# Planning a plain product's weight chunks one product earlier, and loading a 512 KB gain row later, in a two-layer encoder

## The chip, the cores and the metric

The kernel runs on one core of one Trainium2 chip. The metric is the device time of one execution in microseconds. Times of a profile are counted from the start of its span. Engine names are those of the profile: PE (TensorE), DVE (VectorE), ACT (ScalarE), POOL (GpSimd), SP (SyncE, which here only issues loads and stores).

## What is computed

A pre-norm encoder of two layers on 512 tokens of width 1024: in layer 0 two attentions side by side, in layer 1 a neighbourhood attention, and after each a squared-ReLU MLP with a hidden width of 4096. A final RMS norm with a gain row follows. The change touches the MLPs and the final norm:

```python
def sq_relu_mlp(h, w_up, w_down):
    u = jax.nn.relu(h @ w_up)
    return (u * u) @ w_down
...
        h = h + sq_relu_mlp(rmsnorm(h, norm_ffn[layer]), ffn_w_up[layer], ffn_w_down[layer])
    return rmsnorm(h, final_norm)
```

## The kernel before

All matrices are float32. Each operand x is split into a high part (a rounded copy, made by ACT) and a low part (x minus the high part, made by DVE), and a product is three matmuls: high x high, high x low, low x high. A weight chunk arrives from memory in a `raw` tile; its halves are `whi` and `wlo`. The pools have four `raw`, three `whi` and four `wlo` buffers.

**Chunks.** `plan` appends a chunk to a list, and `weights(i)` makes what chunk i needs: it issues the loads of all planned chunks up to i + 5 and makes the halves of all planned chunks up to i + 2. It can only look ahead in what is planned. There are three kinds. `chunk` makes `whi` on ACT (L234) and `wlo` on DVE (L224). `summed_chunk` writes minus the rounded weights to `wlo` on ACT (L261), adds the weights to that by an accumulating load from memory on POOL's queue (L263), and makes `whi` on ACT (L266). `seven_chunk` is for the products below: POOL, for some chunks DVE, forms sums of 128-column blocks (L363 to L365), ACT makes `whi` (L369), DVE makes `wlo` (L370).

**Seven-block products** (`Seven`). A 2 x 2 block product is made of seven block products instead of eight; `run` goes over pairs of row blocks, with 21 matmuls of 256 columns (L457 to L459) for each, and then combines the banks on ACT and DVE (L465 to L469).

**The MLP** (`mlp`). The up projection fills `U`, split activations, and `R`, raw ones; it ends with several seven-block products in `stage`. After each, `finish` squares the result on ACT (L1392, L1393). The down projection has a first part, then `product8`: a plain product over the eight tiles of `U` with the matching weight rows, eight 128-column tiles for each chunk, 24 matmuls of 512 columns (L613 to L615). Its first two chunks are of kind `chunk`, the other six `summed_chunk`. While it runs, `convert` splits the raw activations for the seven-block products that come next, four of seven chunks each (the variable m), in which each result is added to the residual `hT` on DVE (L1592).

In layer 1 there is a last product, `down`, over the remaining four tiles (`last_mlp`), in two halves of 512 output columns with two chunks each. It works with tokens on the partitions and ends in the final norm: `weigh` (L1936) multiplies by the gain row `G`, of which every partition holds a copy: one load of 512 KB (L2065).

**Order.** A program is written engine by engine as a scheduler of the tile library puts the instructions, not strictly as the code is written. Each engine works its own list in order. All raw loads and the gain row are on SP's list, where a load that waits for a buffer holds those behind it. Big tiles come from a list of 32 slots: a slot that is freed goes to its end, and one that is taken comes from its front.

Of the kernel before, what the change touches and what calls it, by code (L numbers as in the profile page):

```python
# [8 lines left out]
F32 = mybir.dt.float32  # L9
# [8 lines left out]
D = 1024  # L18
P = 128
# [16 lines left out]
def encoder_kernel(ctx: ExitStack, tc: tile.TileContext, ins, out, dbg=None):  # L36
    nc = tc.nc
    PE, ACT, DVE, POOL, SP = nc.tensor, nc.scalar, nc.vector, nc.gpsimd, nc.sync
# [50 lines left out]
    def ob():  # L89
        return bank("o", 1)  # L90
# [178 lines left out]
    def rows(w, k0, nk):  # L269
        return w[k0 * P : (k0 + nk) * P, :].rearrange("(k p) n -> p k n", p=P)  # L270
# [6 lines left out]
    def plan(*spec, make=None):  # L277
        asked.append((make or chunk, spec))
        return len(asked) - 1
# [247 lines left out]

        return run()

    def product8(w, first, U, evac, eng=None):  # L530


        nk = len(U)
        ids = [plan([(0, D, rows(w, k, 1))], 1, D, None, eng, make=chunk if n < 2 else summed_chunk)
               for n, k in enumerate(first)]

        def run():
            banks = group(4) + group(4)

            def one(k, j):  # L540

                wh, wl = (z[:, 0, P * j : P * j + P] for z in weights(ids[k], AHEAD - (k == 1 or k == nk - 1 and j < 7)))
                x = U[k].pair()
                mm3(banks[j], wh, wl, x[:, 0, :], x[:, 1, :], k == 0, k == nk - 1)


            for js in (range(4), range(4, 8)):
                for k in (0, 1):
                    for j in js:
                        one(k, j)  # L550
                        yield MM3
            U[0].free()
            U[1].free()
            for k in range(2, nk - 2):
                for j in range(8):
                    one(k, j)
                    yield MM3
                U[k].free()
            for j in range(8):
                for k in (nk - 2, nk - 1):  # L560
                    one(k, j)
                    yield MM3

                if j < 5:
                    evac(j, banks[j])
            for j in range(5, 8):
                tc.keep_in_program_order(evac(j, banks[j]))
            U[nk - 2].free()
            U[nk - 1].free()

        return run()
# [775 lines left out]
    SIZES = (6, 8, 16, 2), (6, 8, 14, 4)  # L1347

    def first_product(l):

        w = ins["ffn_w_up"][l]
# [6 lines left out]
        U, R = [], []  # L1358
# [89 lines left out]
        def ahead():  # L1448
            state["ids"] = x7.plan(w, P * state["c"])

        def stage(n, raw=0, more=0):


            at = [], []
            if not state["plain"]:
                plain()
                at[0].extend(range(0, n, 2))
            nu, nr = (n - len(U)) // 2, raw // 2
            state["n"], state["halves"] = n, raw

            kinds = [1, 0] * nu if nr else [0] * nu
            kinds += [1] * (nr + nu - len(kinds)) + [1] * (more // 2)
            for i, kind in enumerate(kinds):
                ids = state["ids"]
                if i < nu + nr:
                    at[kind].append(state["c"])
                state["c"] += 2
                if i < len(kinds) - 1:
                    ahead()
                for u, _ in enumerate(x7.run(ids, (pair_evac, raw_evac)[kind])):  # L1470
                    if u in (14, 21, 24):
                        next(state["late"], None)
            if state["c"] == 32:
                x7.free()
            got = U[:n], R[: raw // 2], R[raw // 2 :], at, state["late"]
            U.clear()
            R.clear()
            return got
# [41 lines left out]
    def mlp(l, last=None, then=lambda: None):  # L1520
# [4 lines left out]
        stage, ahead, later = first_product(l)  # L1525
# [31 lines left out]
                later(c, i)  # L1557
        for s_ in U:
            s_.free()
        U, R, V, (at_u, at_r), late = stage(*SIZES[l][1:])  # L1560
        first = [k + z for k in at_u for z in range(2)]
        gen = product8(w, first, U, ev)
        u7 = Seven(2 * len(R))
        ids = [u7.plan(w, 256 * m, at_r) for m in range(4)]
        k0 = 32 - 2 * len(V)
# [360 lines left out]
    def last_mlp():  # L1926
# [85 lines left out]
        def down(k0, nk, c, up, tail):  # L2012
# [4 lines left out]
            def run():  # L2017
                banks = group(4)
                if c:
                    banks.append(ob())  # L2020

                def use(k, j, o=0, n=S):
                    wh, wl = (x[:, k % 2, o : o + n] for x in weights(ids[k // 2]))
# [26 lines left out]
        def last(k0, R):  # L2050
            up = []
            runs.extend(down(k0, 2 * len(R), c, up, 2 + 2 * c) for c in range(2))

            def beside(m, i):
                if m == 0 and i % 8 == 4 and R:
                    w_ = R.pop(0)
                    for z in range(2):
                        V.append(Slot())
                        up.append(V[-1].pair())
                        split(w_.t[:, S * z : S * z + S], up[-1])  # L2060
                    w_.free()
                if m == 2 and i == 0:
                    H.extend([Halves(spare_p, F32), Halves(spare_p, F32), Halves(spare_b, F32), Slot(F32)])
                    G.append(Slot(F32))
                    SP.dma_start(G[0].t, ins["final_norm"].unsqueeze(0).to_broadcast([P, D]))  # L2065

            return beside

# [59 lines left out]
```

## Time and profile before

| | us |
|---|---|
| median of 3 runs | 1141.09 |
| lowest, highest | 1140.44, 1141.96 |
| the profiled execution, its own time | 1140.78 |
| its span, first to last instruction | 1139.0 |
| mean granted clock of TensorE | 0.998 |

Rows of a timeline give start, duration, engine, line, operation and tile; in brackets stands how long the engine idled before, and what ended it. PE's rows overlap, since matmuls are pipelined: the distance from start to start is the pace. In a view of waits a row is who waited for whom, us in total, how often, and the longest. In a view of DMAs a row gives the transfers of one kind, their number, KB each and the median us from issue to landing.

### The profile page before, as it was taken

The numbers are of one execution on the slowest core, as the hardware profiler recorded it, in microseconds if no ns is written. First come the engines' busy times: TensorE is split into PE (matmuls) and PEld (weight loads), VectorE is DVE, ScalarE is ACT, GpSimd is POOL, SyncE is SP. The second block draws the span as 40 slices with busy tenths as digits, with TensorE's granted clock in tenths as the row PEclk, the third lists the DMA queues.
The fourth block names the chain that finished last, engine by engine and source line by source line (L and its number), as shares of the span: only waits on it lengthen the run. The fifth ranks groups of instructions, "written<-read, shape, count | busy, mean of one in ns | idle before, by whom it ended". The sixth has DMA issues, their size and how long they took to land.

```text
span 1139.0 us, 20506 instructions
## 1 busy us (share of the span) xinstructions
PE 1124.2 (99%) x7348; PEld 1009.6 (89%) x7348; DVE 904.1 (79%) x1570; ACT 668.3 (59%) x1133; POOL 601.3 (53%) x722
## 2 busy tenths in 40 slices
PE   9999999999999999999999999999999999999997
PEld 7787888888899999899998998988889999989996
DVE  6887997988968787969775666667997788697884
ACT  6677785765347668534464555555552666773334
POOL 4366432226688993378532232221388889535740
PEclk9999999999999999999999999999999999999999
DMA  8322441222533235933585574433344233372332
GB/s 240 98 77 77 117 120 62 65 66 74 169 101 100 86 103 134 277 103 103 160 172 157 149 178 130 119 110 121 102 157 130 76 93 94 80 190 74 113 129 74
DMA packets 118325, 136.06 MB, mean 119 GB/s; under 512 B 9923, under 2 KB 99952, under 8 KB 118224
## 3 DMA queue, kind: packets, MB, share of 16 engines
q1 hardware_dynamic: 110736, 119.83, 34.8%
q0 software_dynamic: 7312, 14.83, 6.8%
q8 instruction: 58, 0.95, 0.4%
q14 instruction: 43, 0.35, 0.1%
q10 hardware_dynamic: 176, 0.10, 0.0%
HBM read 112.70 MB, written 6.29 MB: 104 GB/s over the span
## 4 chain that ended last, share of the span: by engine, by line
PE 82%; DVE 7%; issue 6%; DMA 2%; ACT 2%; POOL 1%; SPq 0%; DVEq 0%; POOLq 0%; ACTq 0%
PE mm L613 9%; PE mm L614 8%; PE mm L615 8%; PE mm L459 3%; PE s L1138 3%; PE mm L457 3%; PE mm L458 3%; PE o L1126 3%; PE t L457 2%; PE t L459 2%; PE t L458 2%; PE t L1113 2%; PE s L615 2%; PE s L613 2%; PE s L614 2%
## 5 line engine op out<-in xcount | busy, mean ns | idle before, releaser
L613 PE MATMUL mm<-a,whi 128*128 128x512 f32 x428 | 172.7, 404 | 0.1
L370 DVE TENSOR_TENSOR wlo<-a,whi 128x896 fp32r<-128x896 f32 x106 | 135.8, 1286 | 43.7 <-ACT whi L369 43.4
L614 PE MATMUL mm<-a,whi 128*128 128x512 f32 x428 | 167.9, 392 | 0.0
L615 PE MATMUL mm<-a,wlo 128*128 128x512 f32 x428 | 167.0, 391 | 0.0
L369 ACT ACTIVATE whi<-a 128x896 fp32r<-128x896 f32 x106 | 100.8, 951 | 96.6 <-PE s L458 23.1
L224 DVE TENSOR_TENSOR wlo<-raw,whi 128x1024 fp32r<-128x1024 f32 (+4 forms) x93 | 105.4, 1139 | 27.1 <-ACT whi L234 26.7
L234 ACT ACTIVATE whi<-raw 128x1024 fp32r<-128x1024 f32 (+3 forms) x96 | 88.1, 919 | 57.0 <-PE s L614 23.2
L459 PE MATMUL mm<-a,wlo 128*128 128x256 f32 x430 | 119.8, 279 | 0.7 <-DVE wlo L370 0.7
L457 PE MATMUL mm<-a,whi 128*128 128x256 f32 x430 | 118.9, 276 | 0.0
L458 PE MATMUL mm<-a,whi 128*128 128x256 f32 x430 | 118.8, 276 | 0.0
L365 POOL TENSOR_TENSOR a<-a 128x128 f32<-128x128 f32 x104 | 100.6, 968 | 8.2
L369 ACT ACTIVATE whi<-raw 128x896 fp32r<-128x896 f32 x58 | 55.2, 955 | 82.5 <-POOL raw L365 22.9
L364 POOL TENSOR_TENSOR a<-a 128x256 f32<-128x256 f32 x104 | 92.6, 890 | 8.1
L615 PEld LDWEIGHTS mm<-a,wlo 128*128 128x128 f32 x428 | 80.4, 188 | 17.1
L1146 POOL TENSOR_SCALAR p<-p,ti 128x512 f32<-128x512 f32 x64 | 47.7, 746 | 88.7 <-DVE ti L1145 67.9
L613 PEld LDWEIGHTS mm<-a,whi 128*128 128x128 f32 x428 | 80.5, 188 | 15.4 <-issue 0.5
L614 PEld LDWEIGHTS mm<-a,whi 128*128 128x128 f32 x428 | 80.7, 189 | 13.5
L1775 POOL TENSOR_SCALAR p<-p,ti 128x256 f32<-128x256 f32 x64 | 35.4, 564 | 104.7 <-DVE ti L1774 91.7
L457 PE MATMUL t<-a,whi 128*128 128x256 f32 x312 | 86.2, 276 | 0.0
L458 PE MATMUL t<-a,whi 128*128 128x256 f32 x312 | 86.2, 276 | 0.0
L459 PE MATMUL t<-a,wlo 128*128 128x256 f32 x312 | 86.1, 276 | 0.0
L370 DVE TENSOR_TENSOR wlo<-raw,whi 128x896 fp32r<-128x896 f32 x58 | 71.5, 1253 | 17.5 <-ACT whi L369 17.5
(449 smaller groups left out, 3594.7 us busy)
## 6 DMA issues: line engine op xcount, KB each, us to landing
a<-in_ffn_w_up_dram SPq DMA_DIRECT2D x102, 256.0 KB, 2.7
raw<-in_ffn_w_down_dram SPq DMA_DIRECT2D x34, 512.0 KB, 4.5
raw<-in_ffn_w_down_dram SPq DMA_DIRECT2D x56, 256.0 KB, 2.7
raw<-in_od_w_qkv_dram SPq DMA_DIRECT2D x64, 128.0 KB, 3.5
raw<-in_ffn_w_up_dram SPq DMA_DIRECT2D x12, 512.0 KB, 3.9
wlo<-in_ffn_w_down_dram POOLq DMA_DIRECT2D x12, 512.0 KB, 6.3
a<-a SPq DMA_DIRECT2D x17, 256.0 KB, 3.4
bx<-a SPq DMA_DIRECT2D x32, 128.0 KB, 5.4
```

Of the source, the lines that this page charges most:

```text
L224: z = lambda: (eng or DVE).tensor_tensor(to, src, f32(high), op=ALU.subtract)
L234: ACT.activation(hi[:, 0:m], raw[:, 0:m], AF.Copy)
L364: held(eng.tensor_tensor(r[:, 4:6], r[:, 2:3].to_broadcast([P, 2, P]), r[:, 0:7:6], op=ALU.add))
L365: held(eng.tensor_tensor(r[:, 7], r[:, 3], r[:, 5], op=ALU.subtract))
L369: ACT.activation(hi, raw[:, 128:1024], AF.Copy)
L370: DVE.tensor_tensor(lo, raw[:, 128:1024], f32(hi), op=ALU.subtract)
L457: PE.matmul(o, wh, x[:, 0], start=kp == 0 and n in (0, 1, 3, 5), stop=False, skip_group_check=True)
L458: PE.matmul(o, wh, x[:, 1], start=False, stop=False, skip_group_check=True)
L459: PE.matmul(o, wl, x[:, 0], start=False, stop=kp == self.np - 1, skip_group_check=True)
L613: PE.matmul(o, wh, xh, start=first, stop=False)
L614: PE.matmul(o, wh, xl, start=False, stop=False)
L615: PE.matmul(o, wl, xh, start=False, stop=last)
```

## The change

There are two edits. First, the planning of `product8`'s eight chunks is taken out of it into `plan8`. `stage` gets a function `then` that it calls ahead of its last seven-block product, and `mlp` gives it `plan8`. So the chunks stand on the list while that product runs, where before they came onto it afterwards. Second, the slot for the gain row is taken, and its load issued, when the first half of the last product (`down` with c = 0) begins, where before this was at the start of the third of the four seven-block products (m = 2).

```diff
--- before.py
+++ after.py
@@ -527,12 +527,15 @@
 
         return run()
 
-    def product8(w, first, U, evac, eng=None):
+    def plan8(w, first, eng=None):
+
+        return [plan([(0, D, rows(w, k, 1))], 1, D, None, eng, make=chunk if n < 2 else summed_chunk)
+                for n, k in enumerate(first)]
+
+    def product8(ids, U, evac):
 
 
         nk = len(U)
-        ids = [plan([(0, D, rows(w, k, 1))], 1, D, None, eng, make=chunk if n < 2 else summed_chunk)
-               for n, k in enumerate(first)]
 
         def run():
             banks = group(4) + group(4)
@@ -1448,7 +1451,7 @@
         def ahead():
             state["ids"] = x7.plan(w, P * state["c"])
 
-        def stage(n, raw=0, more=0):
+        def stage(n, raw=0, more=0, then=None):
 
 
             at = [], []
@@ -1467,6 +1470,8 @@
                 state["c"] += 2
                 if i < len(kinds) - 1:
                     ahead()
+                elif then:
+                    then(at[0])
                 for u, _ in enumerate(x7.run(ids, (pair_evac, raw_evac)[kind])):
                     if u in (14, 21, 24):
                         next(state["late"], None)
@@ -1557,9 +1562,10 @@
                 later(c, i)
         for s_ in U:
             s_.free()
-        U, R, V, (at_u, at_r), late = stage(*SIZES[l][1:])
-        first = [k + z for k in at_u for z in range(2)]
-        gen = product8(w, first, U, ev)
+        ids8 = []
+        U, R, V, (at_u, at_r), late = stage(*SIZES[l][1:], lambda at: ids8.extend(
+            plan8(w, [k + z for k in at for z in range(2)])))
+        gen = product8(ids8, U, ev)
         u7 = Seven(2 * len(R))
         ids = [u7.plan(w, 256 * m, at_r) for m in range(4)]
         k0 = 32 - 2 * len(V)
@@ -2018,6 +2024,9 @@
                 banks = group(4)
                 if c:
                     banks.append(ob())
+                else:
+                    G.append(Slot(F32))
+                    SP.dma_start(G[0].t, ins["final_norm"].unsqueeze(0).to_broadcast([P, D]))
 
                 def use(k, j, o=0, n=S):
                     wh, wl = (x[:, k % 2, o : o + n] for x in weights(ids[k // 2]))
@@ -2061,8 +2070,6 @@
                     w_.free()
                 if m == 2 and i == 0:
                     H.extend([Halves(spare_p, F32), Halves(spare_p, F32), Halves(spare_b, F32), Slot(F32)])
-                    G.append(Slot(F32))
-                    SP.dma_start(G[0].t, ins["final_norm"].unsqueeze(0).to_broadcast([P, D]))
 
             return beside
 
```

The first place is ACT's list at the end of the last seven-block product of layer 1's `stage`. `raw_11848` and `raw_11850` are the first two chunks of `product8`, `raw_11852` and `raw_11857` the next two; `a_11711` is the result that `finish` squares, L424 splits activations. Before:

```order
L369 ACTIVATE whi_11746<-a_11654 128x896
L1392 ACTIVATE a_11711<-a_11711 128x1024
L261 ACTIVATE wlo_11854<-raw_11852 128x1024
L1393 ACTIVATE a_11711<-a_11711 128x1024
L261 ACTIVATE wlo_11859<-raw_11857 128x1024
L234 ACTIVATE whi_11866<-raw_11848 128x1024
L465 ACTIVATE a_11815<-mm_11717 128x256
L234 ACTIVATE whi_11870<-raw_11850 128x1024
L424 ACTIVATE a_11925<-a_10772 128x2x256
L266 ACTIVATE whi_11874<-raw_11852 128x1024
```

Now (the first four of product8's chunks are `raw_11721`, `raw_11723`, `raw_11750`, `raw_11777`; `finish` is at L1395 and L1396):

```order
L369 ACTIVATE whi_11752<-a_11654 128x896
L424 ACTIVATE a_11925<-a_10772 128x2x256
L424 ACTIVATE a_11926<-a_10772 128x256
L234 ACTIVATE whi_11779<-raw_11721 128x1024
L1395 ACTIVATE a_11711<-a_11711 128x1024
L261 ACTIVATE wlo_11808<-raw_11750 128x1024
L1396 ACTIVATE a_11711<-a_11711 128x1024
L234 ACTIVATE whi_11811<-raw_11723 128x1024
L465 ACTIVATE a_11836<-mm_11717 128x256
L266 ACTIVATE whi_11874<-raw_11750 128x1024
L261 ACTIVATE wlo_11871<-raw_11777 128x1024
```

The high half of the first plain chunk (the first L234) has moved from behind the two steps of `finish` and two L261 to ahead of them; the L261 of the fourth chunk has moved from ahead of both L234 to behind the L465 and an L266. In layer 0 the same rows move in the same way.

The second place is DVE's list there, before:

```order
L370 TENSOR_TENSOR wlo_11747<-a_11654,whi_11746 128x896
L224 TENSOR_TENSOR wlo_11867<-raw_11848,whi_11866 128x1024
L466 TENSOR_TENSOR a_11815<-a_11815,mm_11718 128x2x256
L224 TENSOR_TENSOR wlo_11871<-raw_11850,whi_11870 128x1024
L467 TENSOR_TENSOR a_11815<-a_11815,mm_11719 128x512
L425 TENSOR_TENSOR a_11825<-a_10502,a_11825 128x256
L468 TENSOR_TENSOR a_11815<-a_11815,mm_11719 128x256
```

Now:

```order
L370 TENSOR_TENSOR wlo_11753<-a_11654,whi_11752 128x896
L224 TENSOR_TENSOR wlo_11780<-raw_11721,whi_11779 128x1024
L224 TENSOR_TENSOR wlo_11812<-raw_11723,whi_11811 128x1024
L466 TENSOR_TENSOR a_11836<-a_11836,mm_11718 128x2x256
L467 TENSOR_TENSOR a_11836<-a_11836,mm_11719 128x512
L468 TENSOR_TENSOR a_11836<-a_11836,mm_11719 128x256
L469 TENSOR_TENSOR a_11836<-a_11836,s_11720 128x512
```

Both low halves (L224) now stand ahead of the combining of the last seven-block product (L466 to L469), where the second stood between its steps.

The third place is SP's list in the seven-block products of layer 1; `a_12704` is the gain row's slot. Before:

```order
L358 DMA raw_12464<-in_ffn_w_down_dram 128x2x256
L358 DMA raw_12494<-in_ffn_w_down_dram 128x2x256
L2065 DMA a_12704<-in_final_norm_dram 128x1024
L358 DMA raw_12524<-in_ffn_w_down_dram 128x2x256
L358 DMA raw_12554<-in_ffn_w_down_dram 128x2x256
```

Now (L2029 loads the gain row into `a_13117`; L212 loads the chunks of `down`):

```order
L358 DMA raw_12913<-in_ffn_w_down_dram 128x2x256
L358 DMA raw_12943<-in_ffn_w_down_dram 128x2x256
L2029 DMA a_13117<-in_final_norm_dram 128x1024
L212 DMA raw_12973<-in_ffn_w_down_dram 128x2x512
L212 DMA raw_13000<-in_ffn_w_down_dram 128x2x512
```

The gain row's load has moved behind fourteen loads of seven-block chunks and stands just ahead of the four loads of the last product. PE's list is the same in both.

## The prediction

> **What bounds the kernel now.** The page's busy times and chain come first:
>
> ```profile
> PE 1124.2 (99%) x7348; PEld 1009.6 (89%) x7348; DVE 904.1 (79%) x1570; ACT 668.3 (59%) x1133; POOL 601.3 (53%) x722
> PE 82%; DVE 7%; issue 6%; DMA 2%; ACT 2%; POOL 1%; SPq 0%; DVEq 0%; POOLq 0%; ACTq 0%
> ```
>
> TensorE is the bound, and the change neither adds nor removes a matmul. It can only win what TensorE loses while it waits. The view of its waits lists all of that, and four of its ten rows lie in stages that the change touches or could touch:
>
> ```profile
> PE s L459 <- DVE wlo L370: 1.6, 2, 1.4
> ...
> PE s L615 <- DVE wlo L224: 0.9, 2, 0.5
> PE mm L459 <- DVE wlo L370: 0.7, 1, 0.7
> PE s L613 <- ACT whi L234: 0.5, 1, 0.5
> ```
>
> L224 and L234 make the two halves of a weight chunk of a plain product, so the second and fourth rows are the start of the plain product over the first half of the activations (product8), in both layers. The first row's 1.4 us lies in the last layer's seven-block products, where the final norm's row is loaded. The third (0.7 us, first layer) is not touched. That makes everything at stake about 4 us of 1139, or 0.35%; a measurement of this kernel can tell about 0.2% (2.3 us) from no change.
>
> What a wait costs is more than its idle time, so I read TensorE's timeline at the three places, from start to start. First layer, then last layer, then the stall near 1078:
>
> ```profile
> 443.70 0.40 PE L613 MATMUL s<-a,whi 128*128 128x512 f32 x1
> ...
> 444.71 0.50 PE L615 MATMUL s<-a,wlo 128*128 128x512 f32 x1 [0.38 <-DVE wlo L224]
> 445.05 0.39 PE L613 MATMUL t<-a,whi 128*128 128x512 f32 x1
> 445.28 0.40 PE L614 MATMUL t<-a,whi 128*128 128x512 f32 x1
> ```
>
> ```profile
> 991.72 0.28 PE L459 MATMUL s<-a,wlo 128*128 128x256 f32 x1
> 992.53 0.51 PE L613 MATMUL s<-a,whi 128*128 128x512 f32 x1 [0.53 <-ACT whi L234]
> ...
> 993.79 0.50 PE L615 MATMUL s<-a,wlo 128*128 128x512 f32 x1 [0.53 <-DVE wlo L224]
> 994.13 0.40 PE L613 MATMUL t<-a,whi 128*128 128x512 f32 x1
> ```
>
> ```profile
> 1077.62 0.28 PE L458 MATMUL s<-a,whi 128*128 128x256 f32 x1
> 1079.35 0.38 PE L459 MATMUL s<-a,wlo 128*128 128x256 f32 x1 [1.45 <-DVE wlo L370]
> 1079.57 0.29 PE L457 MATMUL t<-a,whi 128*128 128x256 f32 x1
> ```
>
> A 512-wide matmul follows another after 0.23 us (445.05 to 445.28), a 256-wide one after half of that, 0.11. First layer: 443.70 to 445.05 is 1.35 us for three matmuls, where 0.70 would do: **0.65 lost**. Last layer: 991.72 to 994.13 is 2.41, where 0.11 + 0.70 would do: **1.60 lost**. The third place: 1077.62 to 1079.57 is 1.95 for 0.23: **1.72 lost**.
>
> **Part 1, the plan made earlier.** Why the chunk comes late is seen on ScalarE and VectorE:
>
> ```profile
> 985.09 0.94 ACT L369 ACTIVATE whi<-a 128x896 fp32r<-128x896 f32 x1
> 987.63 1.06 ACT L1392 ACTIVATE a<-a 128x1024 f32<-128x1024 f32 x1 [1.59 <-DVE a L469]
> ...
> 991.44 1.04 ACT L234 ACTIVATE whi<-raw 128x1024 fp32r<-128x1024 f32 x1
> ```
>
> ```profile
> 992.51 1.23 DVE L224 TENSOR_TENSOR wlo<-raw,whi 128x1024 fp32r<-128x1024 f32 x1 [3.97 <-ACT whi L234]
> ```
>
> Before its first L234, ScalarE idles 1.59 us and then does L1392, two L261 and L1393 (987.63 to 991.44, 3.8 us); VectorE idles 3.97 us for it. The matmuls could have had the chunk at 991.83. Four seven-block chunks of 21 matmuls (2.38 us each at 0.113) run up to there, so the second of them ends at about 991.83 - 4.76 = 987.1. The high halves have three buffers, so the first plain chunk's can be written from 987.1. In the changed order L234 stands right there, ahead of L1392: done at about 988.1, and L224 (1.23) at about 989.4, in VectorE's idle stretch. The high half is wanted at 991.83 and the low one at 992.3. Both waits go, with 2.9 us to spare. The first layer has the same shape:
>
> ```profile
> 439.49 1.06 ACT L1392 ACTIVATE a<-a 128x1024 f32<-128x1024 f32 x1 [0.70 <-DVE a L469]
> ...
> 442.36 1.04 ACT L234 ACTIVATE whi<-raw 128x1024 fp32r<-128x1024 f32 x1
> ```
>
> There L234 moves ahead of the same group, from 442.36 to about 439.2, and 0.65 goes. Nothing is added: the same operations stand in another order, and no matmul moves.
>
> What is late next? The second plain chunk: L1392, one L261, L1393 and L234 at some 0.96 us each put its high half at 992.0 and its low half at 993.2, wanted at 991.83 + 12 x 0.23 = 994.6. That leaves 1.4 us. The second of the summed chunks loses its place: its L261 goes from ahead of the first L234 to behind L465 and an L266, some 3.5 us later, and its accumulating load on POOL with it.
>
> ```profile
> wlo<-in_ffn_w_down_dram POOLq DMA_DIRECT2D x12, 512.0 KB, 6.3
> ```
>
> Issued at about 995 and landed at 1001.5, it is wanted as the fourth chunk, after three chunks of 24 matmuls: 991.83 + 72 x 0.23 = 1008.4. In the first layer it also stands behind two copies of the bias rows on POOL, some 2 to 3 us more, and is still covered. If that cover went, each us beyond 7 would cost one. So part 1 is **-2.25 us**, with 0 lost elsewhere.
>
> **Part 2, the final norm's row.** Its load, the loads around it, and SP's waits between 1040 and 1115:
>
> ```profile
> 1059.45 0.34 SPq L2065 DMA_DIRECT2D a<-in_final_norm_dram  x1
> ```
>
> ```profile
> SPq L358 <- DVE wlo L370: 33.8, 18, 5.1
> ...
> SPq L2065 <- DVE raw L365: 2.6, 1, 2.6
> ```
>
> The row's load holds SP for 2.6 us, but the raw loads behind it wait for VectorE's L370 on their own account, so the hold costs nothing that I can show. The transfer does have a trace. These are the raw loads issued from 1060.8 to 1064, from 1069.5 to 1072 and from 1073 to 1095, each from the DMA view of its window, and the row itself:
>
> ```profile
> raw<-in_ffn_w_down_dram SPq DMA_DIRECT2D x3, 256.0 KB, 2.9
> ```
>
> ```profile
> q8 instruction: 1, 0.02, 3.5%
> ...
> raw<-in_ffn_w_down_dram SPq DMA_DIRECT2D x2, 256.0 KB, 3.9
> ```
>
> ```profile
> raw<-in_ffn_w_down_dram SPq DMA_DIRECT2D x8, 256.0 KB, 2.6
> ```
>
> ```profile
> a<-in_final_norm_dram SPq DMA_DIRECT2D x1, 512.0 KB, 3.7
> ```
>
> With the row in flight three raw loads land 0.3 us late. The two that feed the stall took 3.9, and in their window stands an instruction load (q8), not the row, which had landed by 1063.15. Then VectorE:
>
> ```profile
> 1074.93 0.83 DVE L363 TENSOR_TENSOR raw<-raw 128x128 f32<-128x128 f32 x1 [0.82 <-DMA raw<-in_ffn_w_down_dram]
> ...
> 1078.21 2.62 DVE L370 TENSOR_TENSOR wlo<-raw,whi 128x896 fp32r<-128x896 f32 x2
> ```
>
> L363 starts when the second of those loads is in; L469, L364, L1592 and L365 follow without a gap, and then the L370 that TensorE waits for. So the stall comes mostly from the 3.9 us loads. The row's share is indirect: without it everything up to those loads runs 0.3 us sooner, and being issued 0.3 us sooner, more of their packets get ahead of the instruction load. Bounds: 0 (the instruction load sets it alone) and 1.72 (all of it; the waits list no such stall at the product boundaries before and after). I take **-0.7**, 0.3 counted twice, nearer to the row 2.9 against 2.6 than to the whole stall.
>
> At its new place the row is held until the third product's addition (L1592) is done, by the built program's wait. It starts at 1093.44 and takes 1.21, so the load goes out near 1094.7. The raw loads of the seven blocks are through by then, and the last product's four loads follow from 1096.15:
>
> ```profile
> L1592 DVE TENSOR_TENSOR hT<-hT,a x4: 1210/1212/1224, 1058.2 to 1109.3; 128x1024 f32<-128x1024 f32 x4
> ```
>
> ```profile
> 1093.44 1.21 DVE L1592 TENSOR_TENSOR hT<-hT,a 128x1024 f32<-128x1024 f32 x1
> ```
>
> ```profile
> 1096.15 1.91 SPq L212 DMA_DIRECT2D raw<-in_ffn_w_down_dram  x2
> ```
>
> ```profile
> 1102.06 1.22 DVE L224 TENSOR_TENSOR wlo<-raw,whi 128x1024 fp32r<-128x1024 f32 x1 [1.34 <-ACT whi L234]
> ```
>
> ```profile
> 1106.31 0.39 PE L2029 MATMUL s<-wlo,a 128*128 128x512 f32 x1
> ```
>
> The first low half is ready at 1103.28 and wanted at 1106.31: 3.0 us of slack. If the 512 KB delayed the first chunk by its whole 3.7 us, 0.7 would be lost; if by the 0.3 seen above, nothing. I take 0. [...]
>
> **Sum.** -0.65 - 1.60 - 0.7 = -2.95 us against the profiled execution's 1140.78 (span 1139.0 and 1.78 around it): 1137.8. The median of the runs, 1141.09, is 0.31 above that execution, so a median of **1138.1**.
>
> **Rivals.** (a) The move of the row wins nothing: the instruction load and VectorE's evacuation set that stall. For it: the 3.9 us loads come 6 us after the row landed. 1141.09 - 2.25 = 1138.8, on the bound of 0.2%. (b) The stall near 1078 goes whole: with slightly sooner loads the instruction load falls between two of them. For it: neighbouring boundaries have no such wait. 1141.09 - 3.97 = 1137.1. (c) A new wait takes the place of those removed: the second plain chunk (1.4 us of slack), or the last product's first chunk (0.7 at worst), gives back about 1: 1139.1 to 1139.8. Against it: both slacks are larger than any shift seen. (d) Slower: the row's load waits for a buffer freed later, that of the fourth product's addition (1109.3 + 1.21 = 1110.5), and the four loads queue behind it on SP. Its first chunk would be ready at 1110.5 + 3.7 + 1.06 + 1.22 = 1116.5, 10 us after it is wanted: 1141.09 - 2.25 + 10 = about 1149. It decides as soon as the release comes after 1098. Against it: the built program waits for the third. (e) That the plan moves and the instructions don't is ruled out by the order of ScalarE.
>
> **How the numbers follow.** Forecast 1138.1 (1137.4 to 1138.7): 0.46. (a) 0.25, (b) 0.15, (c) 0.10, (d) 0.04. Faster by over 0.2% means under 1138.8: the forecast, (b) and a little under a third of (a), 0.68. Within it: the rest of (a) and nearly all of (c), 0.28. Slower: 0.04. The range reaches from (b) with 0.5 of scatter, as the three runs of before lie up to 0.9 from their median, to (c): 1136.6 to 1139.8.
>
> **What would show it.** The waits of TensorE for L224 and L234 at the head of product8 are gone in both layers, and VectorE's idle 3.97 us is cut short; if one stays, part 1's order of buffers was misread. The stall near 1078 is shorter but there, and raw loads at that place land in 2.6 us: if it is unchanged, (a), if gone, (b). The row is issued near 1092 on the new clock and the last product starts without a wait; a wait there is (c) or (d). I am wrong above all if an instruction load falls on another raw load at a boundary and makes a stall where none was.

## The result, and the profile after

| | before | after |
|---|---|---|
| median, us (18 runs each) | 1140.62 | 1137.95 |
| lowest to highest | 1137.97 to 1142.95 | 1135.21 to 1139.93 |
| the profiled execution, its own time | 1140.78 | 1137.52 |
| its span | 1139.0 | 1135.7 |
| mean granted clock | 0.998 | 0.998 |

The ratio is 0.9977, 95% interval 0.9969 to 0.9985: 2.7 us faster, between 1.7 and 3.5. Forecast were 1138.1 and a gain of 2.95. In the changed kernel L613 to L615 are L616 to L618, L1392/L1393 are L1395/L1396, L1592 is L1598, SP's L2065 (the row) is L2029 and PE's L2029 is L2038; L224 to L469 keep their numbers.

TensorE's waits after the change (who waited for whom, total, times, longest) have no L224 and no L234 any more. The 1.4 us for L370 is still there:

```profile
PE s L459 <- DVE wlo L370: 1.4, 1, 1.4
...
PE mm L459 <- DVE wlo L370: 0.9, 1, 0.9
```

TensorE's timeline at the start of product8, first layer, then last layer:

```profile
442.25 0.40 PE L616 MATMUL s<-a,whi 128*128 128x512 f32 x1
...
442.94 0.40 PE L616 MATMUL t<-a,whi 128*128 128x512 f32 x1
```

```profile
990.35 0.28 PE L459 MATMUL s<-a,wlo 128*128 128x256 f32 x1
990.47 0.40 PE L616 MATMUL s<-a,whi 128*128 128x512 f32 x1
...
991.16 0.40 PE L616 MATMUL t<-a,whi 128*128 128x512 f32 x1
```

442.25 to 442.94 is 0.69 and 990.35 to 991.16 is 0.81, the pure pace (0.69, and 0.11 + 0.69). The reason is seen on ScalarE and VectorE in the last layer:

```profile
985.89 1.05 ACT L234 ACTIVATE whi<-raw 128x1024 fp32r<-128x1024 f32 x1
986.84 1.04 ACT L1395 ACTIVATE a<-a 128x1024 f32<-128x1024 f32 x1
...
989.68 1.04 ACT L234 ACTIVATE whi<-raw 128x1024 fp32r<-128x1024 f32 x1
```

```profile
987.51 1.22 DVE L224 TENSOR_TENSOR wlo<-raw,whi 128x1024 fp32r<-128x1024 f32 x1
990.76 1.23 DVE L224 TENSOR_TENSOR wlo<-raw,whi 128x1024 fp32r<-128x1024 f32 x1 [2.03 <-ACT whi L234]
```

The first L234 stands ahead of L1395. Its high half is there at 986.94 and the low half at 988.73, wanted at 990.47 and 990.93. The second chunk's low half is there at 991.99; after twelve matmuls of the first it is wanted at 990.47 + 12 x 0.23 = 993.2 at the earliest. VectorE's idle 3.97 us ahead of the first low half is gone, and 2.03 us stand ahead of the second.

The boundary between two seven-block products near 1078 of the old clock, in the new:

```profile
1074.61 0.28 PE L458 MATMUL s<-a,whi 128*128 128x256 f32 x1
1076.25 0.38 PE L459 MATMUL s<-a,wlo 128*128 128x256 f32 x1 [1.37 <-DVE wlo L370]
1076.47 0.29 PE L457 MATMUL t<-a,whi 128*128 128x256 f32 x1
```

1074.61 to 1076.47 is 1.86 for 0.23: 1.63 is lost, where it was 1.72. So this stall is hardly shorter. A smaller one stood at the next boundary, too short for the view of waits to list, and the prediction had none there. Before:

```profile
1096.18 0.39 PE L459 MATMUL mm<-a,wlo 128*128 128x256 f32 x1
1096.40 0.28 PE L457 MATMUL mm<-a,whi 128*128 128x256 f32 x1
```

Here 0.22 us lie between two starts, and 17 matmuls take 2.12 us; after the change they take 1.93, at 0.11 each.

All matmuls have the same order in both programs, so that their starts can be compared one by one. The change took 0.65 us at product8 of the first layer, 1.60 at that of the last, 0.08 at the boundary near 1078 and 0.19 at the next one, 2.5 in sum. The two profiled executions differ by 3.26. The remaining 0.7 lies in stretches with the same instructions in the same order (1.46 gained before the first product8, 0.74 given back between the two). With part 1 alone, below, the same early stretch is 0.3 slower than before, so this is scatter between executions.

### The profile page after: what moved, and what is told of

Its sections match the earlier page's. It is cut to its first block, busy times and chain, and to the rows that moved or that the text cites. A ratio compares the mean times of both kernels' runs of the same rounds, so it can differ in the third digit from the quotient of the medians.

```text
span 1135.7 us, 20510 instructions
## 1 busy us (share of the span) xinstructions
PE 1122.8 (99%) x7348; PEld 1009.4 (89%) x7348; DVE 903.6 (80%) x1570; ACT 668.0 (59%) x1133; POOL 599.7 (53%) x722
## 4 chain that ended last, share of the span: by engine, by line
PE 81%; issue 5%; DVE 5%; DMA 5%; POOL 2%; ACT 1%; SPq 1%; POOLq 0%; DVEq 0%; ACTq 0%
PE mm L616 8%; PE mm L617 8%; PE mm L618 8%; PE mm L459 3%; PE mm L457 3%; PE mm L458 3%; PE s L1141 3%; PE o L1129 3%; DMA raw<-in_ffn_w_down_dram 2%; PE t L459 2%; PE t L457 2%; PE t L458 2%; PE t L1116 2%; PE s L616 2%; PE s L617 2%
## 5 line engine op out<-in xcount | busy, mean ns | idle before, releaser
L616 PE MATMUL mm<-a,whi 128*128 128x512 f32 x428 | 172.7, 404 | 0.1
L370 DVE TENSOR_TENSOR wlo<-a,whi 128x896 fp32r<-128x896 f32 x106 | 135.2, 1281 | 43.6 <-ACT whi L369 43.2
L618 PE MATMUL mm<-a,wlo 128*128 128x512 f32 x428 | 167.0, 391 | 0.0
L224 DVE TENSOR_TENSOR wlo<-raw,whi 128x1024 fp32r<-128x1024 f32 (+4 forms) x93 | 105.5, 1141 | 24.7 <-ACT whi L234 24.4
L234 ACT ACTIVATE whi<-raw 128x1024 fp32r<-128x1024 f32 (+3 forms) x96 | 88.1, 919 | 56.7 <-PE s L617 23.1
L618 PEld LDWEIGHTS mm<-a,wlo 128*128 128x128 f32 x428 | 80.4, 188 | 17.1
L616 PEld LDWEIGHTS mm<-a,whi 128*128 128x128 f32 x428 | 80.5, 188 | 15.4 <-issue 0.5
L370 DVE TENSOR_TENSOR wlo<-raw,whi 128x896 fp32r<-128x896 f32 x58 | 70.9, 1243 | 18.5 <-ACT whi L369 18.5
```

The lines of the kernel that those rows point to most:

```text
L224: z = lambda: (eng or DVE).tensor_tensor(to, src, f32(high), op=ALU.subtract)
L234: ACT.activation(hi[:, 0:m], raw[:, 0:m], AF.Copy)
L370: DVE.tensor_tensor(lo, raw[:, 128:1024], f32(hi), op=ALU.subtract)
L616: PE.matmul(o, wh, xh, start=first, stop=False)
L618: PE.matmul(o, wl, xh, start=False, stop=last)
```

## The experiments

Each group of runs is compared with runs of the kernel before that were taken beside it, so the time of before differs from group to group.

**One part at a time.** plan_only has the first edit and loads the row at its old place; row_only has the second edit and plans as before.

```diff
 row_only (against the changed kernel)
-        def stage(n, raw=0, more=0, then=None):
+        def stage(n, raw=0, more=0):
...
-        gen = product8(ids8, U, ev)
+        gen = product8(w, first, U, ev)
 plan_only (against the changed kernel)
-                else:
-                    G.append(Slot(F32))
-                    SP.dma_start(G[0].t, ins["final_norm"]...)
...
                 if m == 2 and i == 0:
+                    G.append(Slot(F32))
+                    SP.dma_start(G[0].t, ins["final_norm"]...)
```

> Part 1 alone: the plan is made earlier, the gain row stays where it was before. Theory (all of the gain is the two waits at the head of product8): TensorE's waits for L224 and L234 there are gone, worth 0.65 + 1.60 = 2.25 us in its timeline, and the stall near 1078 on the old clock stays at 1.5 to 1.7; time 2.0 to 2.6 us below before. Rival (the row's move carries a good part of the measured 2.7): the time is less than 1.8 us below before.

> Part 2 alone: the gain row is loaded when the last product begins, the plan is as before. Theory: both waits at the head of product8 stay (2.25 us), the stall near 1078 keeps at least 1.4 of its 1.72 us because the load for the fifth chunk still lands over 4 us late beside an instruction load; time 0 to 0.4 us below before. Rival (the prediction's term): the stall falls to about 1.0 us, time 0.7 us below before. Rival of the other sign: the four loads of the last product land later and TensorE waits at its start, time above before.

Measured against 1140.74: plan_only 1138.84, ratio 0.9983 (0.9971 to 0.9995); row_only 1139.85, ratio 0.9994 (0.9984 to 1.0003). TensorE's start of product8 in the last layer, plan_only and row_only:

```profile
991.16 0.40 PE L616 MATMUL s<-a,whi 128*128 128x512 f32 x1
...
991.63 0.39 PE L618 MATMUL s<-a,wlo 128*128 128x512 f32 x1
```

```profile
991.78 0.50 PE L613 MATMUL s<-a,whi 128*128 128x512 f32 x1 [0.49 <-ACT whi L234]
...
993.04 0.50 PE L615 MATMUL s<-a,wlo 128*128 128x512 f32 x1 [0.53 <-DVE wlo L224]
```

Part 1 wins both waits by itself (0.65 and 1.60 by the starts of the matmuls). Part 2 leaves the last layer's in place. In the first layer row_only loses 0.29 rather than 0.65, though all its instructions there are those of before: this wait varies by itself between executions.

At the boundary near 1078, plan_only loses 1.59 and row_only 1.42, against 1.71 before. The interval of row_only holds both no gain and the 0.7 that the prediction gave it; its trace, of one execution, shows 0.30 less at this boundary and 0.19 less at the next one. Beside part 1, the row's move did less: the stall is 1.59 without it (plan_only) and 1.64 with it (the changed kernel), and 0.24 goes at the next boundary (2.17 for the 17 matmuls, then 1.93).

**Loads found earlier, and sums taken off VectorE.** What sets that stall? res2 lets the last layer's chunks take one more of the big slots for their raw loads; dve2 gives the sums of the sixth chunk to GpSimd, as those of most chunks are.

```diff
 res2
-        reserve[0] = 3 if last else 2
+        reserve[0] = 2
 dve2
-            ... DVE if pairs and c0 and kp in (2, 5) else None,
+            ... DVE if pairs and c0 and kp in (2,) else None,
```

> The changed kernel with one slot less held in reserve in the last layer's seven-block products, so that some weight chunks go to free slots and are loaded without waiting for one of the four raw buffers. Theory (late loads of the fifth chunk make the stall at the product boundary): those loads are issued earlier, the stall of 1.5 us falls below 0.5, time 1 to 1.5 us below the changed kernel. Rival (VectorE's combining of the finished product stands ahead of the fifth chunk's low half and sets the stall): stall over 1.2 us, time within 0.4 us of the changed kernel.

> The changed kernel with the sixth chunk's block sums on GpSimd in place of VectorE, in both layers, which takes about 2 us of work out of VectorE's list at each product boundary. Theory (the late load sets the stall): the load for the fifth chunk still lands over 4 us late, its low half can begin when its high half is there, about 1 us earlier than now: stall 0.3 to 1.0 us. Rival (VectorE's list alone sets the stall): stall gone, under 0.2. Third case: GpSimd becomes late with the block sums and new waits appear, time above the changed kernel.

res2: 1139.95, ratio 0.9998 (0.9989 to 1.0006). It lost 1.2 us more in small waits between 1042 and 1073, and 1.59 at the boundary, though the raw load issued 4.8 us ahead of it lands in 2.58; the stall of under 0.5 that its theory expected did not come. VectorE's list is another there (L466 begins 4.9 us ahead of the boundary, in the changed kernel 7.2), so this run does not tell the theories apart.

dve2: 1139.76, ratio 0.9995 (0.9986 to 1.0003). The boundary loses 1.13 rather than 1.63, which is neither of the two sizes expected, and new waits of about 1.1 each stand near 554 and 1096, the third case of its text. So VectorE's list has a part in the stall, and taking sums off it makes another chunk late.

**Another phase of the instruction loads.** The two raw loads that feed the stall land late (4.28 and 3.72 us in the changed kernel) beside an instruction load, a transfer that the profile lists as "instruction" on queue q8: 58 of them, of 16 KB, for 7348 matmuls and 7348 weight loads, 253 each. It is taken for TensorE's, since in the changed kernel 193 to 303 matmuls and weight loads start between two of them, over 13.2 to 29.3 us. The raw loads issued from 1066 to 1067 and from 1067 to 1069 in the changed kernel (number, KB, median us to landing; q8's share is of 16 engines' time, so 4.6% of 2 us is 1.5 us on one of them):

```profile
raw<-in_ffn_w_down_dram SPq DMA_DIRECT2D x1, 256.0 KB, 4.3
```

```profile
q8 instruction: 1, 0.02, 4.6%
...
raw<-in_ffn_w_down_dram SPq DMA_DIRECT2D x1, 256.0 KB, 3.7
```

More or fewer matmuls at the program's start, with results nobody uses, move the instruction loads against the work and nothing else in the order of the engines that matter here.

```diff
     idle_work(8)
+    pad = ob()
+    for _ in range(32):      # 64, 96
+        PE.matmul(pad[:, 0:2], ones, ones[:, 0:2], start=True, stop=True)
```

> The changed kernel with 32 two-column matmuls more at its very start (their result is not used); nothing else differs on TensorE. They are 64 instructions more (32 weight loads, 32 matmuls), so that each later instruction load of TensorE comes about 3.6 us earlier against the work: near 1064 rather than near 1067.4 of the changed kernel's clock. Theory (the stall at the product boundary near 1077 comes from an instruction load that shares the time of two raw loads): the two raw loads that feed that boundary land in 2.6 to 3.1 us rather than 4.28 and 3.72, and the stall falls from 1.4 to under 0.7 us; another boundary may get one. Rival (VectorE's own list, with the finished product's sum ahead of the low half, makes it): the stall stays at 1.2 us or more with loads of 2.6.

> As before with 64 matmuls more at the start: TensorE's instruction loads come about 7 us earlier against the work, near 1060.3 and 1075.3. Theory: the raw loads of the boundary near 1077 land in 2.6 to 3.1 us, the stall there under 0.7 us. Rival: 1.2 us or more. If the raw loads beside the instruction load at its new place still take about 4.2 us, the collision is a property of the instruction load and not of the place; both theories allow that.

> As before with 96 matmuls more at the start: TensorE's instruction loads come about 10.8 us earlier (or 4 us later) against the work, near 1056.6 and 1071.6. Theory: the loads of the boundary near 1077 land in 2.6 to 3.1 us unless one of them is still in flight at 1071, the stall there under 0.7 us. Rival: 1.2 us or more. Together the three runs and the changed kernel give four phases: by the theory the stall at that boundary goes with the landing time of its raw loads, by the rival it does not.

Two things in these texts were wrong. Such a product is two matmuls and two weight loads on TensorE (x7412 rather than x7348 for 32), so the shift is twice what they say, and 64 of them, 256 instructions, are about a whole period. And the start lies on the path: the times are 1156.07, 1163.56 and 1182.68 (one execution each), which says nothing of the stall. At the boundary 1.32, 0.40 and 0.95 are lost, in this order.

```diff
-    idle_work(8)
+    idle_work(4)             # 2
```

> The changed kernel with 4 rather than 8 of the matmuls on ones at its start, whose result nobody uses: 8 matmuls and 8 weight loads fewer, so that TensorE's instruction loads come about 0.9 us later against the work. Theory (the phase of the instruction load against the raw loads sets the stall near 1076): the load at 1067.4 comes at 1068.3, 2 us behind the first of the two raw loads, which then lands in 2.6 to 3.2 us rather than 4.28; 0.4 to 1.2 us less is lost there, and the time is 1136.8 to 1137.6, unless another boundary gets a collision. Rival: the stall stays at 1.2 us or more, 1137.9.

> As before with 2 rather than 8: 12 matmuls and 12 weight loads fewer, the instruction loads about 1.4 us later. Theory: the load comes at 1068.8, as in the run with 64 matmuls more, where it came at 1069.1 and no stall was left: 1.0 to 1.5 us less is lost near 1076, time 1136.5 to 1137.2 unless another boundary gets a collision. Rival: the stall stays at 1.2 us or more, 1137.9. At the start the first matmul on data must not come later than 4.71 us; if it does, the matmuls left out were of use there and that much is to be set against the gain.

idle4: 1139.66, ratio 0.999 (0.998 to 1.0). idle2: 1140.1, ratio 0.9998 (0.9987 to 1.0009). In idle4 the two loads (issued from 1069 to 1071 and from 1071 to 1074) are on time, the instruction load falling between them, and TensorE passes the boundary with 0.31 lost:

```profile
raw<-in_ffn_w_down_dram SPq DMA_DIRECT2D x1, 256.0 KB, 2.6
```

```profile
q8 instruction: 1, 0.02, 2.3%
...
raw<-in_ffn_w_down_dram SPq DMA_DIRECT2D x1, 256.0 KB, 2.8
```

```profile
1078.53 0.28 PE L458 MATMUL s<-a,whi 128*128 128x256 f32 x1
1078.85 0.39 PE L459 MATMUL s<-a,wlo 128*128 128x256 f32 x1
```

Set against the matmuls, on the clock of the changed kernel, the instruction load came at 1067.4 in the changed kernel and at 1068.2 in idle4. But in before and in kept_last (below), which have all matmuls at the start, it came at 1068.1 and 1068.3, with loads of over 4 us. So the eight matmuls fewer do not by themselves explain idle4. What differs there is that its two loads were issued 8.9 and 6.4 us ahead of the boundary, where the changed kernel's were issued 8.3 and 7.1 ahead; why they were is not settled here.

In idle2 the instruction load comes at 1069.7 on that clock, 2.3 us after the second load's issue; that load takes 4.58 and 1.80 is lost, against its expectation. Neither kernel is faster than the changed one, and both miss the times expected: the starts lose 1.1 and 0.9 (below), and in idle4 a like wait of 1.5 us stands at 491.84 of the first layer, where VectorE's list is held by a late load:

```profile
488.56 0.75 DVE L363 TENSOR_TENSOR a<-a 128x128 f32<-128x128 f32 x1 [3.50 <-DMA a<-in_ffn_w_down_dram]
```

All runs with the same order on VectorE in one table, worked out from their timelines. Times are against the last matmul ahead of the awaited low half; "list" is from the landing of the second load to the end of the first L370:

| run | two loads, us to landing | second in, us ahead | list, us | lost, us |
|---|---|---|---|---|
| before | 4.33, 3.48 | 2.72 | 4.39 | 1.71 |
| plan_only | 4.19, 3.35 | 2.85 | 4.38 | 1.59 |
| row_only | 4.17, 3.62 | 3.56 | 4.93 | 1.42 |
| after | 4.28, 3.72 | 3.34 | 4.93 | 1.64 |
| shift32 | 2.63, 2.82 | 3.09 | 4.36 | 1.32 |
| shift96 | 2.62, 2.71 | 3.22 | 4.13 | 0.95 |
| shift64 | 2.85, 3.75 | 3.63 | 3.98 | 0.40 |
| idle4 | 2.61, 2.78 | 3.61 | 3.88 | 0.31 |
| idle2 | 2.64, 4.58 | 2.64 | 4.39 | 1.80 |

The loss is the list less the lead of the second load, within 0.1 us in every row. That holds by construction, since TensorE goes on when the awaited low half is there; what the table adds is which of the two parts moves. In shift32 and shift96 the loads take 2.6 to 2.8, and still 1.32 is lost, as the rival said, and 0.95, which neither text expected: there they are issued 1.1 us later, since the loads ahead of them met the instruction load (4.25 and 3.69 in shift32), VectorE's list waited for those, and the buffers came free later. So the theory of the phase is right about where the lateness comes from, and only half of the story: the other half is a list of 4 to 5 us.

**Why the list grew.** The second load is in 0.62 us earlier after the change, as the prediction had counted (0.3 twice), and the list takes 0.54 more. In the first four rows of the table the longer list goes with the row's move: 4.93 in the two kernels with it, 4.39 and 4.38 in the two without. VectorE's list after the change, and the two rows of before that differ:

```profile
1071.29 0.83 DVE L363 TENSOR_TENSOR raw<-raw 128x128 f32<-128x128 f32 x1 [1.05 <-DMA raw<-in_ffn_w_down_dram]
1072.04 0.67 DVE L469 TENSOR_TENSOR a<-a,s 128x512 f32<-128x512 f32 x1
1072.64 0.41 DVE L364 TENSOR_TENSOR raw<-raw 128x256 f32<-128x256 f32 x1
1072.97 1.48 DVE L1598 TENSOR_TENSOR hT<-hT,a 128x1024 f32<-128x1024 f32 x1
1074.37 0.82 DVE L365 TENSOR_TENSOR raw<-raw 128x128 f32<-128x128 f32 x1
1075.12 2.34 DVE L370 TENSOR_TENSOR wlo<-raw,whi 128x896 fp32r<-128x896 f32 x2
```

```profile
1076.61 1.21 DVE L1592 TENSOR_TENSOR hT<-hT,a 128x1024 f32<-128x1024 f32 x1
1077.75 0.54 DVE L365 TENSOR_TENSOR raw<-raw 128x128 f32<-128x128 f32 x1
```

These two rows take 0.27 and 0.28 more. GpSimd's sums of the seventh chunk run beside them, after and before:

```profile
1072.64 0.73 POOL L363 TENSOR_TENSOR raw<-raw 128x128 f32<-128x128 f32 x1
1073.45 1.59 POOL L364 TENSOR_TENSOR raw<-raw 128x256 f32<-128x256 f32 x1
```

```profile
1076.61 1.53 POOL L363 TENSOR_TENSOR raw<-raw 128x128 f32<-128x128 f32 x1 [0.46 <-DMA raw<-in_ffn_w_down_dram]
```

Before, GpSimd's first sum begins with VectorE's addition and takes 1.53, twice the 0.73 of after, and VectorE keeps its 1.21. After, GpSimd is already at work when the addition begins, and VectorE pays. copy7 replaces GpSimd's three sums of the seventh chunk by one copy on ScalarE, so those block sums are left out of the result:

```diff
-        held(eng.tensor_tensor(r[:, 6], r[:, 0], r[:, 1], op=ALU.subtract))
...
+        if eng is ACT:
+            held(ACT.activation(raw[:, 512:1024], raw[:, 0:512], AF.Copy))
...
-            ... DVE if pairs and c0 and kp in (2, 5) else None,
+            ... {2: DVE, 5: DVE, 6: ACT}.get(kp) if pairs and c0 else None,
```

> The changed kernel with GpSimd's three sums of the seventh chunk (products with columns behind the first ones) replaced by one copy of the same 512 columns on ScalarE: those block sums are left out of the result. Theory (VectorE's addition of the finished product and its third sum run long there because GpSimd's sums run beside them): at the boundary near 1076 the addition takes 1.21 us rather than 1.48 and the third sum 0.54 rather than 0.82; from the landing of the second raw load to the end of the awaited low half 4.4 us rather than 4.93, and 0.5 us less is lost (1.0 rather than 1.53). Rival (the two durations have another reason, or only the landing decides): they stay at 1.48 and 0.82, or the loss stays at 1.4 or more.

Its addition and third sum at the boundary (line numbers 3 higher):

```profile
1073.20 1.21 DVE L1601 TENSOR_TENSOR hT<-hT,a 128x1024 f32<-128x1024 f32 x1
1074.34 0.28 DVE L368 TENSOR_TENSOR raw<-raw 128x128 f32<-128x128 f32 x1
```

The list is 4.15 rather than 4.93 with the second load 3.29 us ahead, and 0.91 is lost rather than 1.64. So GpSimd's sums cost the list 0.5 us (after against before) to 0.8 us (against copy7). The kernel ran once, in 1136.91, which is too little to tell a gain.

**The order of the list.** The awaited L370 belongs to a chunk whose sums were done long before. It stands behind L363, which waits for a raw load that is needed three chunks later, and behind what follows it. sums_kept holds VectorE's sums in the written order, behind the finished product's additions, with the L370 ahead of the last two sums; kept_last does so in the last layer alone. Nothing else moves on any engine.

```diff
 sums_kept
-        held = (lambda z: z) if eng else tc.keep_in_program_order
+        held = tc.keep_in_program_order
 kept_last
+        held = (lambda z: z) if eng and reserve[0] == 2 else tc.keep_in_program_order
```

> The changed kernel with VectorE's three sums of a chunk (L363 to L365) kept in the written order behind the finished product's additions, in both layers; nothing else differs on any engine. At the boundary near 1076 the list reads L469, addition, L363, L370, L364, L365: the low half that TensorE awaits belongs to a chunk whose sums were done long before, and it stood behind L363, which waits for a raw load needed only three chunks later. Theory (the stall needs both, a late landing and the order of VectorE's list): wherever the instruction load falls, the awaited L370 ends about 0.83 (L363) + 1.08 (L370) = 1.9 us after the landing of the second raw load rather than 4.93, so about 1.4 us behind the last matmul before the boundary turns into no wait; 1.2 to 1.5 us less is lost there and the first layer's like boundaries lose no more than now: time 1136.2 to 1137.0. Rival (the landing alone decides): the stall stays at 1.0 us or more while its raw loads land in 3.5 to 4.3, time 1137.7 to 1138.2. A third way: sums done later make another chunk late, and a wait appears three chunks behind a boundary; then the time is above 1138.

> As the run before, but the three sums are kept behind the additions in the last layer alone; the first layer has the order of the changed kernel, so that the wait of 0.6 us near 538 is not there. Theory (a late landing hurts only through VectorE's order): no wait at the boundary near 1076 whether its raw loads land in 2.6 or in 4.3 us, 1.3 to 1.5 us less lost there than in the changed kernel; up to 0.5 given back near 1093; ratio to before 0.9963 to 0.9970 (time about 1136.8 to 1137.4). Rival (the place is right, but the time goes into small losses elsewhere, as in the run before): ratio 0.9971 to 0.9979, the changed kernel's.

sums_kept: 1137.87 against 1140.82, ratio 0.9971 (0.9961 to 0.9981). kept_last: 1138.29 against 1141.51, ratio 0.9972 (0.9961 to 0.9984). The loads issued from 1066 to 1069 in kept_last meet the instruction load as before, VectorE's list has the new order, and TensorE goes through:

```profile
q8 instruction: 1, 0.02, 2.1%
...
raw<-in_ffn_w_down_dram SPq DMA_DIRECT2D x2, 256.0 KB, 4.2
```

```profile
1071.49 1.32 DVE L1598 TENSOR_TENSOR hT<-hT,a 128x1024 f32<-128x1024 f32 x1
1072.73 0.83 DVE L363 TENSOR_TENSOR raw<-raw 128x128 f32<-128x128 f32 x1
1073.48 1.08 DVE L370 TENSOR_TENSOR wlo<-raw,whi 128x896 fp32r<-128x896 f32 x1
1074.48 0.68 DVE L364 TENSOR_TENSOR raw<-raw 128x256 f32<-128x256 f32 x1
```

```profile
1074.72 0.28 PE L458 MATMUL s<-a,whi 128*128 128x256 f32 x1
1074.84 0.28 PE L459 MATMUL s<-a,wlo 128*128 128x256 f32 x1
```

With loads of 4.2 us (second one in 2.9 us ahead), nothing is lost at the boundary, in both kernels. The place is settled: landings as late as these cost time here only through the order of VectorE's list. The time is not: both ratios' intervals overlap the changed kernel's 0.9969 to 0.9985, and both missed the time that the theory expected (kept_last lies where its rival put it). In the profile of sums_kept 0.8 us is given back at 538.6 (L370 behind the delayed sums), 0.5 at 1093.4, and the rest in pieces of 0.1 to 0.3. kept_last has no wait at 538, gives back 0.7 after the boundary, and its profiled execution, 1136.71, is 0.81 below the changed kernel's, which is less than runs scatter. No version here is shown to beat the changed kernel.

## Why the prediction came out as it did

**Part 1: right in mechanism and size.** 2.25 was forecast; the starts of the matmuls give 0.65 + 1.60 = 2.25 both in the changed kernel and for part 1 alone, whose median is 1.9 us lower (ratio interval 0.6 to 3.3 us). That it fits to the hundredth is luck, as row_only's 0.29 for the first layer shows. L234 was to stand at 987.1 on the old clock; 985.89 is 987.2 there (product8's first matmul was due at 991.83, and comes at 990.47). The slack was smaller for the low half (2.2 rather than 2.9) since L224 starts behind an L370, and 1.2 rather than 1.4 for the second chunk. The summed chunk that lost its place delayed nothing: TensorE has no wait for it.

**Part 2: right direction, mis-sized, and won at another place.** The term was -0.7, all of it at the stall near 1078. Alone, the row's move measured 0.30 there and 0.19 at the next boundary. Beside part 1, as the sum used it, it measured nothing at the stall (1.59, then 1.64) and 0.24 at the next boundary. The step "0.3 counted twice" held in its sum up to the landing (0.62 earlier, 0.84 in row_only), but by luck: the second load was issued 0.86 earlier against the boundary, and it took 3.72 rather than 3.48, so no part was won by packets that get ahead of the instruction load. The step that failed is the next one, that the rest of VectorE's list follows at its old durations: begun earlier it ran into GpSimd's sums, which took back 0.54. Rival (a) was right for this term by its result. Its reason, that the instruction load and VectorE's evacuation set the stall, is what the runs show, but the two as factors of one sum, and VectorE's part is the order of its list more than its length. Rival (b), the stall gone by an instruction load that falls between two raw loads, did not happen here; idle4, where the instruction load began as the second raw load was issued, shows that it can. That raw loads at the stall would land in 2.6 was wrong: they took 4.28 and 3.72.

**The new place of the row: right.** SP's row, the four loads behind it after and before, and the last product's first low half:

```profile
1091.19 0.34 SPq L2029 DMA_DIRECT2D a<-in_final_norm_dram  x1
```

```profile
raw<-in_ffn_w_down_dram SPq DMA_DIRECT2D x4, 512.0 KB, 5.0
```

```profile
raw<-in_ffn_w_down_dram SPq DMA_DIRECT2D x4, 512.0 KB, 4.9
```

```profile
1098.77 1.23 DVE L224 TENSOR_TENSOR wlo<-raw,whi 128x1024 fp32r<-128x1024 f32 x1 [1.34 <-ACT whi L234]
```

```profile
1103.02 0.39 PE L2038 MATMUL s<-wlo,a 128*128 128x512 f32 x1
```

The row went out at 1091.19, the low half is there at 1100.0 and wanted at 1103.02: 3.0 us of slack, as before. Rivals (c) and (d) did not occur. The four loads lost 0.1 us in the median.

The row, put ahead of the four loads, did not delay the first of them by its whole time. That load took 3.56 and 3.47 us in before and plan_only, where the row had gone out long before; with the row issued 1.5 us ahead it took 3.64 in the changed kernel and 4.27 in row_only, and with the row 1.2 us ahead 5.24 in copy7. So the first load took up to 1.7 us longer, less than the row's whole 3.7 (its time to landing in before; 3.3 in the changed kernel), and the slack covered it.

**The total.** 2.5 by the places against 2.95 forecast, and 2.7 by the medians. That the median came within 0.2 us of 1138.1 is partly luck: the median of before is 0.47 lower over the 18 runs than over the three that the prediction had, which covers the 0.28 by which the gain fell short.

## What to carry to other kernels

A wait that a load seems to cause is a sum: when the data landed, and what the in-order list between the landing and the awaited instruction holds. Work out both, and ask which instruction in the list needs data that is not wanted yet: an instruction behind it pays for that load. When a step is made earlier, take the durations of what follows from a place where its new neighbours run too, since here an addition on VectorE took 1.48 us with GpSimd already at its sums (the changed kernel) and 1.21 without them (copy7), and a sum on GpSimd took 0.73 where it began ahead of that addition and 1.53 where it began with it (before).

## What the runs showed of the hardware

- **An instruction load can make a 256 KB load in flight late.** In the runs of the table a raw load took 3.7 to 4.3 us rather than 2.6 where TensorE's 16 KB instruction load began about 1 us after its issue (1.1 us in the changed kernel; 4.58 in idle2, where it began 2.3 us after), and in the first four rows the one issued behind it 3.3 to 3.7. Not every meeting costs: in idle4 one began just as the second load was issued, and that load took 2.78. TensorE itself shows no cost: in the changed kernel the instruction loads that begin at 1039.7, 1053.2, 1067.4, 1083.6 and 1100.1 leave no two matmuls over 0.6 us apart between 1030 and 1112 but at the boundary. One instruction load goes with 253 matmuls and weight loads in the mean, and 128 matmuls and 128 weight loads more (shift64) put the one at the boundary back to nearly the same place, at 1068.4 on the matmuls' clock, where before has 1068.1 and the changed kernel 1067.4. So the price falls on other transfers. Why a load is late then was not tried.
- **VectorE and GpSimd.** In before, where VectorE's addition of 128 x 1024 and GpSimd's 128 x 128 sum both begin at 1076.61, the addition took 1.21 and the sum 1.53. In the changed kernel, where the sum begins 0.33 us ahead of the addition, the sum took 0.73 and the addition 1.48. In copy7, without GpSimd's sums there, the addition took 1.21 again. Why they slow each other was not shown.
- **The first matmuls, whose result nobody uses, are worth their time.** With 8 of them fewer on TensorE (idle4), the first matmul on data starts 0.15 us sooner (4.56 rather than 4.71), but three 512-wide matmuls a little later take 1.65 us rather than 0.96. In the changed kernel first, then in idle4:

```profile
6.43 0.96 PE L897 MATMUL mm<-a,whi 128*128 128x512 f32 x3 [0.17 <-ACT a L661]
7.23 0.60 PE L655 MATMUL t<-cst,a 128*128 128x128 f32 x4
7.59 0.94 PE L897 MATMUL mm<-a,wlo 128*128 128x512 f32 x3
8.37 0.86 PE L897 MATMUL mm<-a,whi 128*128 128x512 f32 x3
```

```profile
6.70 1.65 PE L897 MATMUL mm<-a,whi 128*128 128x512 f32 x3 [0.42 <-ACT a L661]
8.15 1.06 PE L655 MATMUL t<-cst,a 128*128 128x128 f32 x4
8.86 1.51 PE L897 MATMUL mm<-a,wlo 128*128 128x512 f32 x3
10.20 0.87 PE L897 MATMUL mm<-a,whi 128*128 128x512 f32 x3
10.91 0.60 PE L655 MATMUL t<-cst,a 128*128 128x128 f32 x4
```

  By 10.9 us idle4 is 1.1 us behind. The granted clock shows 1.00 in both for these stretches, so it doesn't show this. The pace from start to start does: in idle4 three 512-wide matmuls take 1.45 us from 6.70 and 1.34 from 8.86, in the changed kernel 0.80 from 6.43 and 0.78 from 7.59. The three from 10.20 in idle4 take 0.71, so the faster pace came there between 8.9 and 10.2 us. What sets the pace was not shown.
